# Retention states computed a head ahead, and three projections left beside the first attention scores, in a one-core hybrid transformer layer

## The chip, the core and the metric

The kernel runs on one core of a Trainium2 chip. A core has a matrix engine (PE, with its own weight loader PEld), three engines for elementwise work (VectorE or DVE, ScalarE or ACT, GpSimd or POOL), a queue that issues most transfers (SyncE or SP), and 16 DMA engines. Every engine works through its own list of instructions in order and waits on semaphores. On-chip memory has 128 partitions; PE writes only into PSUM, eight banks of 128x512 32-bit values. The metric is device time in microseconds (us) of one execution.

## What is computed

One layer of a diffusion backbone: 1024 latent tokens and 256 context tokens of width 1024, everything in 32-bit floating point.

```python
h_lat = rms_norm(x, norm1_g) * (1 + sc1) + sh1          # and h_ctx from the context
rq, rk, rv, rg, dq, dk, dv = split(h @ w_in)            # 7 blocks of 512 columns
# retention: 4 heads, 2 directions, chunks of 128 tokens
scores = (qc @ kc.T) * intra
o = scores @ vc + (qc * q_dec) @ S
S = S * c_dec + (kc * k_dec).T @ vc
y_ret = silu(rg) * sum(group_norm(o, gn_g[d]) for d in (0, 1))
# differential attention: 4 heads, two score maps each
a = softmax(q1 @ k1.T) - lam * softmax(q2 @ k2.T)
y_diff = rms_norm(a @ v) * subln_g * (1 - lambda_init)
x = x + g1 * (concat(y_ret, y_diff) @ w_out)
x = x + g2 * (conv3(h2 @ w_up) gated @ w_down);  out = rms_norm(x) * final_g
```

The context's state comes first in each direction, so a latent chunk's state S depends on all chunks before it (direction 0) or behind it (direction 1).

## The kernel before

**Large products.** A 32-bit operand is split into a high and a low part; `passes` (L126) multiplies high by high, high by low and low by high, so a tile of 128x512 results over a depth of 1024 takes 24 matmuls, called passes here. Function `natural` (L387) makes tiles with tokens on the partitions, `transposed` (L442) tiles with features on the partitions. A block of `w_in` is streamed in four slices, split by ACT (`whi`) and DVE (`wlo`, L183).

**Order of the blocks.** dv (block 6), dk (5), rv (2), rk (1), rg (3), rq (0), dq (4). After a tile of q or k, `rotated` (L415) applies the rotary position code: ACT copies the tile to `xb` with the halves of each rotated group exchanged, DVE forms `xa = tile*cos`, `xb*sin`, and their sum. For heads of 64 features the exchange goes in four copies of 32 partitions, for 128 in two of 64. `split_store` (L408) then splits a dk or dq tile (`xhl`: a cast by ACT, a subtraction by DVE) and stores it to memory (`dq_d`, `dk_d`).

**Side work.** `beside(g, rate, due)` hangs a generator of small steps next to the large products: `tick` (L376) is called after each group of three passes, adds `rate`, and takes a step of the generator for each whole unit. A scheduler may still move single instructions; the built order is fixed on each engine.

**Retention.** Beside block 3, `states_before` (L318) computes the direction-1 states of all four heads (nine products `pub` a head, DVE accumulates them into `Sb`). Beside blocks 0 and 4, `outputs` (L351) runs 32 steps (4 heads x 8 chunks). A step's instructions are spread over several iterations: POOL scales the query for both directions (`qq`, L256) and the key (`ks`, L231); PE forms the scores `pc` (L272); DVE masks them (`sc`, L274); PE forms the output `po` (four matmuls, L279 and L280) and the state product `puf` (L291), which DVE adds to the running direction-0 state `Sf` (L238) that the next step's `po` needs; ACT copies `po` to `o` and sums its squares (L282, L286); DVE adds the epsilon (`ss`, L114) and POOL raises to -0.5 (L115); DVE scales `o` twice (L297); POOL adds the directions and applies the gate (`y`, L299, L300); PE turns `y` (`pyt`, L304), ACT and DVE split it (`yr`, L309, L310), and every second step a transfer writes `yrd`.

**Attention.** A unit is one head and 128 queries, 32 in all. For each of its two score maps: six matmuls into `pA` (three banks, one such buffer for a map), a minimum over 1280 keys by DVE (`mt`, L731), an exponential by ACT (`p`, L735). Then DVE forms a ratio and combines the maps in place (L743); PE transposes ten blocks (`pt`), ACT copies them (`aT`), PE multiplies with the values (`pv`, L760, ten instructions that each show as two). The list `TAU` orders the operations of overlapping units, and `in_order` (L117) fixes that order on PE, DVE, ACT and SP. Below, a *score set* is one unit's six score matmuls for one map.

**The seam.** All retention steps are drained before the last `TAIL = 2` products of block 4. The buffers of the attention lie where the retention's lay, so the first loads `qhl`, `ks` (keys of head 0, in four parts, those of map 1 first) and `va`, issued by POOL, wait for the last `yrd` transfer. Unit 0's early operations (`EARLY`) stand in the program ahead of the last two products; their order is left to the scheduler.

Of the kernel before, what the change touches and what calls it, by code (L numbers as in the profile page):

```python
# [60 lines left out]
TAIL = 2  # L61
EARLY = ("S1", "M1", "S0", "M0", "E1", "E0", "R", "C")
# [10 lines left out]
def kernel(  # L73
# [63 lines left out]
    dq_d = [dr.tile([2, 64, 2, L], F32, name=f"dq{h}") for h in range(H)]  # L137
    dk_d = [dr.tile([2, 64, 2, LK], F32, name=f"dk{h}") for h in range(H)]
# [13 lines left out]
    with ExitStack() as p1:  # L152
# [8 lines left out]
        ps_b = psx.enter_context(tc.tile_pool(name="psb1", bufs=3, space=PSUM))  # L161
        mm_tiles = itertools.cycle([ps_b] * 3 + [ps_a] * 2)

        def mm_tile(name):
            return next(mm_tiles).tile([P, 512], F32, name=name, tag="mm")
# [52 lines left out]
        def load_kvg(h, g, nm, n, bufs=4):  # L218
            kvg = rt.tile([P, 2 if nm == "c" else 3, 2, P], F32, name=f"kvg{nm}", bufs=bufs)
            nc.sync.dma_start(out=kvg[:, :n], in_=kvg_d[g][:, :n, :, h * P : (h + 1) * P])  # L220
            return kvg
# [6 lines left out]

        def kscale(k1, h, d):
            kk = rt.tile([P, P], F32, name=f"ks{d}")  # L230
            nc.gpsimd.tensor_scalar(out=kk, in0=k1, scalar1=kd[:, h, d : d + 1], scalar2=0.0, op0=ALU.mult, op1=ALU.add)  # L231
            return kk

        def state_step(dst, prev, pu, h, d):
            if prev is None:
                nc.vector.tensor_copy(dst, pu)
            else:
                nc.vector.scalar_tensor_tensor(out=dst, in0=prev, scalar=cd[:, d * H + h : d * H + h + 1], in1=pu, op0=ALU.mult, op1=ALU.add)  # L238

        class Step:  # L240
            def __init__(self, n):
                self.h, self.t = divmod(n, NT)
                h, t = self.h, self.t
                if t % 2 == 0:
# [3 lines left out]
                    steps["pair"] = (qk, load_kvg(h, t // 2 + 1, "f", 3))  # L248
                qk, kvg = steps["pair"]
                self.qT, self.kT = (qk[:, i, t % 2 * P : (t % 2 + 1) * P] for i in range(2))  # L250
                self.kn, self.v, self.sg = (kvg[:, i, t % 2, :] for i in range(3))
                self.S = None
# [3 lines left out]
                nc.gpsimd.tensor_tensor(out=self.qq, in0=self.qT.unsqueeze(1).to_broadcast([P, 2, P]), in1=qd[:, h], op=ALU.mult)  # L256

            def first_state(self):
                ctx, kk = steps["ctx"]
                pu = pst.tile([P, NTC, P], F32, name="puc", tag="tr")  # L260
                for c in range(NTC):
                    mm(pu[:, c, :], kk[:, c, :], ctx[:, 1, c, :], start=True, stop=True)
# [558 lines left out]
        for op in EARLY:  # L821
            units[0].run(op)
# [556 lines left out]
```

## Time and profile before

| what | us |
|---|---|
| median of 3 runs | 1448.55 |
| lowest and highest | 1448.17, 1450.31 |
| the profiled execution | 1441.0 |
| its span, from first to last instruction shown | 1439.2 |
| block 3 with the direction-1 states | 288 to 342 |
| blocks 0 and 4 with the 32 retention steps | 342 to 497 |
| attention's score and value products | 494 to 693 |

Stages are told by the source lines of the PE instructions. A row of a timeline gives start, duration, engine, line, operation, result and operands, a count, and in brackets the idle time just before it with what ended it. A row of windows gives for each engine the busy time in a stretch, then the granted PE clock (1.00 is full), the DMA engines' busy share and the rate in GB/s.

### The profile page before, as it was taken

To read this page: it belongs to the slowest core of one execution; us is meant where nothing else is said; L and a number is where in the kernel's file an instruction comes from. 1 tells how busy PE (TensorE), PEld (TensorE's weight loads), DVE (VectorE), ACT (ScalarE), POOL (GpSimd) and SP (SyncE) were. 2 spreads that over 40 slices of the span, in tenths; PEclk is the share of its full clock that TensorE was granted. 3 is DMA by queue.
4 is the path that set the end of the run, shared out by engine and by line. 5 is a ranking of instruction groups with operands and counts; after the bars stand their busy time and mean duration, and the time that the engine had idled before them with its cause. 6 is when DMAs were issued, how large, how long until landed. Compare 5 with 4: busy or idle time off the path is not lost.

```text
span 1439.2 us, 19420 instructions
## 1 busy us (share of the span) xinstructions
PE 1379.9 (96%) x6924; PEld 1141.9 (79%) x6924; DVE 1003.8 (70%) x1493; ACT 732.4 (51%) x1394; POOL 340.8 (24%) x451
## 2 busy tenths in 40 slices
PE   6999999999899899999999899999999999999996
PEld 2678787887777789999888677888888888888885
DVE  3565655333677598888346888878777777998457
ACT  3535512322456688998224655555555545455533
POOL 1210000022787323431002253322223230000001
PEclk9999999999999999999999999999999999999999
DMA  8557655466455767480511123223222224953224
GB/s 332 199 194 240 219 196 190 137 193 195 134 173 164 208 156 164 121 143 1 220 62 78 59 104 118 108 110 110 92 87 93 110 110 174 391 206 102 101 95 176
DMA packets 107673, 218.30 MB, mean 152 GB/s; under 512 B 8948, under 2 KB 47348, under 8 KB 106680
## 3 DMA queue, kind: packets, MB, share of 16 engines
q1 hardware_dynamic: 99448, 192.14, 38.3%
q0 software_dynamic: 8128, 24.91, 7.7%
q8 instruction: 55, 0.90, 0.3%
q14 instruction: 42, 0.34, 0.1%
HBM read 159.61 MB, written 57.41 MB: 151 GB/s over the span
## 4 chain that ended last, share of the span: by engine, by line
PE 66%; DVE 8%; DMA 5%; POOL 3%; issue 3%; ACT 3%; SPq 0%; POOLq 0%; DVEq 0%; ACTq 0%
PE chain L129 5%; PE pv L760 5%; PE chain L130 5%; PE pA L728 5%; PE chain L131 5%; PE c L131 4%; PE c L129 4%; PE c L130 4%; PE third L130 2%; PE third L129 2%; PE third L131 2%; DMA W<-w_down 2%; PE pt L748 2%; PE pn L130 2%; PE pn L131 2%
## 5 line engine op out<-in xcount | busy, mean ns | idle before, releaser
L129 PE MATMUL chain<-T,whi 128*128 128x512 f32 x264 | 103.8, 394 | 4.9 <-ACT T L941 3.3
L129 PE MATMUL pl<-hT,whi 128*128 128x512 f32 x256 | 107.1, 419 | 0.0
L130 PE MATMUL chain<-T,whi 128*128 128x512 f32 x264 | 103.2, 391 | 0.0
L131 PE MATMUL chain<-T,wlo 128*128 128x512 f32 x264 | 102.6, 390 | 0.0
L131 PE MATMUL pl<-hT,wlo 128*128 128x512 f32 x256 | 100.5, 393 | 0.0
L130 PE MATMUL pl<-hT,whi 128*128 128x512 f32 x256 | 100.5, 393 | 0.0
L731 DVE TENSOR_REDUCE mt<-pA 128x1 f32<-128x1280 f32 x64 | 95.3, 1490 | 3.3 <-PE pA L728 1.5
L728 PE MATMUL pA<-ks,qhl 128*128 128x512 f32 (+1 forms) x384 | 91.6, 375 | 4.7 <-ACT p L735 4.7
L1024 POOL TENSOR_TENSOR cmb<-wrb 128x512 f32<-128x512 f32 x22 | 36.2, 1647 | 243.2 <-DMA wrb<-w_up 141.3
L131 PE MATMUL c<-whi,ghl 128*128 128x512 f32 x232 | 90.4, 390 | 0.2 <-DVE ghl L1183 0.2
L130 PE MATMUL c<-wlo,ghl 128*128 128x512 f32 x232 | 90.3, 389 | 0.0
L129 PE MATMUL c<-whi,ghl 128*128 128x512 f32 x232 | 90.2, 389 | 0.0
L115 POOL TENSOR_TENSOR sm<-sm,mhalf 128x1 f32<-128x1 f32 x26 | 16.1, 621 | 304.7 <-DVE sm L114 301.4
L735 ACT ACTIVATE p<-pA,mt 128x1280 f32<-128x1280 f32 x64 | 85.5, 1336 | 4.6 <-DVE mt L731 4.5
L894 ACT CAST whi<-cmb 128x512 fp32r<-128x512 f32 x66 | 41.0, 622 | 83.5 <-PE chain L130 63.7
L728 PEld LDWEIGHTS pA<-ks,qhl 128*128 128x128 f32 x384 | 68.9, 193 | 17.5 <-ACT p L735 5.8
L129 PE MATMUL pn<-whi,hT 128*128 128x512 f32 x192 | 79.1, 412 | 0.0
L760 PE MATMUL pv<-va,aT 128*128 128x128 f32 x640 | 77.0, 275 | 0.1
L131 PE MATMUL pn<-whi,hT 128*128 128x512 f32 x192 | 75.9, 398 | 0.5 <-DVE hT L540 0.5
L130 PE MATMUL pn<-wlo,hT 128*128 128x512 f32 x192 | 76.1, 396 | 0.0
L895 DVE TENSOR_TENSOR wlo<-cmb,whi 128x512 fp32r<-128x512 f32 x66 | 60.7, 922 | 20.2 <-ACT whi L894 20.2
L760 PEld LDWEIGHTS pv<-va,aT 128*128 128x128 f32 x640 | 74.0, 192 | 0.7 <-DVE yT L789 0.3
(301 smaller groups left out, 3884.1 us busy)
## 6 DMA issues: line engine op xcount, KB each, us to landing
wm<-w_mod SPq DMA_DIRECT2D x32, 512.0 KB, 4.4
raw<-w_in SPq DMA_DIRECT2D x28, 512.0 KB, 4.4
wra<-w_up SPq DMA_DIRECT2D x24, 512.0 KB, 3.2
wrb<-w_up SPq DMA_DIRECT2D x24, 512.0 KB, 3.5
W<-w_down SPq DMA_DIRECT2D x44, 256.0 KB, 6.4
ad<-s SPq DMA_DIRECT2D x20, 512.0 KB, 3.4
wra<-ad SPq DMA_DIRECT2D x20, 512.0 KB, 3.2
wrb<-ad SPq DMA_DIRECT2D x18, 512.0 KB, 3.3
```

The lines of the kernel that those rows point to most:

```text
L115: nc.gpsimd.tensor_tensor(out=out_ap, in0=out_ap, in1=mhalf[:, :n], op=ALU.pow)
L129: mm(ps, lh, rh, start=first, stop=False, skip_group_check=more)
L130: mm(ps, lh, rl, start=False, stop=False, skip_group_check=more)
L131: mm(ps, ll, rh, start=False, stop=last, skip_group_check=more)
L728: mm(self.pa[m][:, c0:c1], self.q[:, i, m, qs], self.k[:, m, c0:c1], start=(i == 0), stop=(i == 1))
L731: nc.vector.tensor_reduce(out=self.mt[:, m : m + 1], in_=self.pa[m][:, :LK], axis=AX.X, op=ALU.min)
L735: nc.scalar.activation(self.p[m], self.pa[m][:, :LK], AF.Exp, scale=-1.0, bias=self.mt[:, m : m + 1], accum_out=self.s[:, m : m + 1])
L748: nc.tensor.transpose(self.pt[g][:, i, :], self.p[0][:, (4 * g + i) * P : (4 * g + i + 1) * P], ident)
L760: mm(self.pv, self.aT[:, c, :], self.v[:, c, :], start=(c == 0), stop=(c == NKT - 1))
L894: nc.scalar.copy(hi, src)
L895: nc.vector.tensor_tensor(out=lo, in0=src, in1=r32(hi), op=ALU.subtract)
L1024: nc.gpsimd.tensor_tensor(out=s1, in0=b1, in1=b2, op=ALU.add)
```

## The change

**States.** `states_before` and the running direction-0 state are replaced by `states(h)`: 18 products of one head, both directions in turn, each chunk pair's keys and values loaded for each direction (`kvs`), keys scaled two chunks at a time (`ks`, 128x256). Heads 0 and 1 run beside block 3, head 2 during the steps of head 1, head 3 during those of head 2. The number of state products is unchanged (72), and so is that of scores, outputs and turns.

**Steps.** `outputs` scores two steps ahead instead of one (`qq` and `sc` get three buffers), has no state product of its own, loads values and gates alone, and DVE's epsilon instruction goes to POOL. The rate beside the products becomes 1.5 a tick after a delay of 21. PSUM: the three banks `psb1` are split into two more for the small results (five in all) and one for products (three in all).

**Seam.** `TAIL` is 3. The early operations of units 0 and 1 hang on the ticks of the last three products by the table `AHEAD`, and `in_order` fixes this stretch too. The load of the second half of head 0's queries waits for unit 1's combine.

**Exchange.** The host stores the columns of dq and dk with the two maps interleaved, so that the exchange is always two copies of 64 partitions; the memory layout of `dq_d`, `dk_d` and the rotary tables follow.

```diff
-TAIL = 2
-EARLY = ("S1", "M1", "S0", "M0", "E1", "E0", "R", "C")
+TAIL = 3
+EARLY = ("S1", "M1", "E1", "S0", "M0", "E0", "R", "C")
+AHEAD = {15: [(0, op) for op in EARLY[:3]], 18: [(0, op) for op in EARLY[3:6]], 22: [(1, op) for op in EARLY[:3]], 23: [(0, op) for op in EARLY[6:]], None: [(1, op) for op in EARLY[3:]]}
...
-                if t < NT - 1:
-                    self.kk = kscale(self.kn, h, 0)
-                self.qq = rt.tile([P, 2, P], F32, name="qq")
+                self.qq = rt.tile([P, 2, P], F32, name="qq", bufs=3)
...
-                rsqrt(self.ss, self.ss, 1.0, GN_EPS * P, 2)
-
-            def update(self, nxt):
-                pu = pst.tile([P, P], F32, name="puf", tag="tr")
-                mm(pu, self.kk, self.v, start=True, stop=True)
-                nxt.S = rt.tile([P, P], F32, name="Sf")
-                state_step(nxt.S, self.S, pu, self.h, 0)
+                nc.gpsimd.tensor_scalar(out=self.ss, in0=self.ss, scalar1=1.0, scalar2=GN_EPS * P, op0=ALU.mult, op1=ALU.add)
+                nc.gpsimd.tensor_tensor(out=self.ss, in0=self.ss, in1=mhalf[:, :2], op=ALU.pow)
...
+        def states(h):
+
+            seq = [(0, 0, (0, 1)), (1, 0, (1, 0))]
+            for g in range(1, 5):
+                seq += [(0, g, (0, 1) if g < 4 else (0,)), (1, 5 - g, (1, 0) if g < 4 else (1,))]
...
+                nc.gpsimd.tensor_scalar(out=ks, in0=kv[:, 0], scalar1=kd[:, h, d : d + 1], scalar2=0.0, op0=ALU.mult, op1=ALU.add)
...
+                for c in cs:
+                    pu = tr_tile([P, P], "pu")
+                    mm(pu, ks[:, c, :], kv[:, 1, c, :], start=True, stop=True)
...
+                        nc.vector.scalar_tensor_tensor(out=dst, in0=last[d], scalar=cd[:, d * H + h : d * H + h + 1], in1=pu, op0=ALU.mult, op1=ALU.add)
+                    last[d] = dst
+                    yield
...
-            for n in range(-2, n_steps + 4):
-                new = 0 <= n + 1 < n_steps
-                if new:
-                    steps[n + 1] = Step(n + 1)
-                    steps[n + 1].score()
+            lead = 2
+            more = iter(())
+            for n in range(-lead, n_steps + 4):
+                if n + lead < n_steps:
+                    steps[n + lead] = Step(n + lead)
+                    steps[n + lead].score()
...
+                if n == NT:
+                    more = states(2)
+                if n == 2 * NT:
+                    more = states(3)
...
+                for _ in range(3 if n % NT < 6 else 0):
+                    if next(more, more) is None:
+                        yield
...
-            for q in range(P // blk):
-                o = (q ^ 1) * blk
-                nc.scalar.activation(xb[q * blk : (q + 1) * blk, :], pt[o : o + blk, :], AF.Copy, scale=scale)
+            for q in (0, 64):
+                nc.scalar.activation(xb[q : q + 64, :], pt[64 - q : P - q, :], AF.Copy, scale=scale)
...
-        beside(outputs(), 1.2, -12.0)
+        beside(outputs(), 1.5, -21.0)
...
-        for op in EARLY:
-            units[0].run(op)
+        units[1] = Unit(1)
+        vars(units[1]).update(fore[1])
+
+        def prologue():
+            for k in range(8 * TAIL):
+                for u, op in AHEAD.get(k, ()):
+                    units[u].run(op)
+                yield
+
+        start = len(nc.cur_bb.bb.instructions)
+        beside(prologue(), 1.0)
         transposed(wg, dq_d, rtab, 32, -DIFF_SCALE, 0, by_head[-TAIL:])
+        for u, op in AHEAD[None]:
+            units[u].run(op)
+        in_order(start)
...
-                with tc.issue_after(units[n - 5].pool_ins.ins) if n >= 5 else nullcontext():
+                after = units[n - 5].pool_ins if n >= 5 else units[1].joined if n else None
+                with tc.issue_after(after.ins) if after else nullcontext():
                     fore.append(load(n + 3))
```

**POOL in the retention steps.** One step's instructions as they stand in a run of steps of head 0, before (from one power of -0.5, `ss<-ss,mhalf`, to the next):

```order
L115 TENSOR_TENSOR ss<-ss,mhalf 128x2
L299 TENSOR_TENSOR y<-o 128x128
L300 TENSOR_TENSOR y<-y,kvgf 128x128
L256 TENSOR_TENSOR qq<-qk,qd 128x256
L231 TENSOR_SCALAR ks_3241<-kvgf,kd 128x128
```

and now, at the border of head 0 and head 1, where the scaling of keys for head 2 begins:

```order
L267 TENSOR_SCALAR ss<-ss 128x2
L268 TENSOR_TENSOR ss<-ss,mhalf 128x2
L274 TENSOR_TENSOR y<-o 128x128
L275 TENSOR_TENSOR y<-y,kvo 128x128
L248 TENSOR_TENSOR qq<-qk,qd 128x256
L305 TENSOR_SCALAR ks<-kvs,kd 128x256
```

The epsilon instruction is new on POOL, the scaled keys are fewer and twice as wide; the first `y` still stands right behind the power of its own step.

**DVE at the seam.** `mt` is the minimum for one score set, `xa`, `xb`, `xhl` belong to the last two dq products, `p` is a unit's combine. Before, from unit 0's first minimum to unit 1's second (`pA_4584` and `pA_4592` are unit 0's maps 1 and 0, `pA_4711` and `pA_4721` unit 1's):

```order
L731 TENSOR_REDUCE mt_4582<-pA_4584 128x1
L412 TENSOR_TENSOR xhl_4642<-xa_4633,xhl_4642 128x512
L739 RECIPROCAL r_4604<-sa_4583 128x1
L731 TENSOR_REDUCE mt_4582<-pA_4592 128x1
L423 SCALAR_TENSOR_TENSOR xa_4671<-pl_4646,rtab_3830 128x512
L424 TENSOR_TENSOR xb_4672<-xb_4672,rtab_3830 128x512
L731 TENSOR_REDUCE mt_4709<-pA_4711 128x1
L740 SCALAR_TENSOR_TENSOR r_4604<-r_4604,sa_4583,nlam_145 128x1
L425 TENSOR_TENSOR xa_4671<-xa_4671,xb_4672 128x512
L743 SCALAR_TENSOR_TENSOR p0_4602<-p1_4600,r_4604,p0_4602 128x1280
L412 TENSOR_TENSOR xhl_4680<-xa_4671,xhl_4680 128x512
L731 TENSOR_REDUCE mt_4709<-pA_4721 128x1
```

and now, from behind unit 0's first minimum and the rotation of the product before the last, to unit 1's second minimum (`pA_4562` is unit 0's map 0, `pA_4584` and `pA_4612` unit 1's maps 1 and 0, `pA_4656` unit 2's map 1):

```order
L396 TENSOR_TENSOR xhl_4548<-xa_4541,xhl_4548 128x512
L720 TENSOR_REDUCE mt_4466<-pA_4562 128x1
L720 TENSOR_REDUCE mt_4468<-pA_4584 128x1
L728 RECIPROCAL r_4597<-sa_4467 128x1
L729 SCALAR_TENSOR_TENSOR r_4597<-r_4597,sa_4467,nlam_145 128x1
L732 SCALAR_TENSOR_TENSOR p0_4570<-p1_4539,r_4597,p0_4570 128x1280
L406 SCALAR_TENSOR_TENSOR xa_4601<-pl_4552,rtab_3750 128x512
L407 TENSOR_TENSOR xb_4602<-xb_4602,rtab_3750 128x512
L720 TENSOR_REDUCE mt_4654<-pA_4656 128x1
L408 TENSOR_TENSOR xa_4601<-xa_4601,xb_4602 128x512
L396 TENSOR_TENSOR xhl_4608<-xa_4601,xhl_4608 128x512
L720 TENSOR_REDUCE mt_4468<-pA_4612 128x1
```

Unit 0's second minimum has moved behind the rotation of the product before the last, and unit 1's second minimum now stands behind unit 2's first as well as behind the last product's rotation. On PE the score sets are unit 0's two and unit 1's map 1, with 9, 12 and 3 passes of the last product behind them; before, unit 0's map 1 alone stood ahead of the last ten passes.

More of the change, by code (lines that the diff above doesn't have):

```diff
@@ L253, in __init__ @@
[L253 to L268 removed]
+                self.v, self.sg = (kv[:, i, t % 2, :] for i in range(2))
@@ L302, in turn @@
             def turn(self):
-                pt = pst.tile([P, P], F32, name="pyt", tag="tr")
+                pt = tr_tile([P, P], "pyt")
                 nc.tensor.transpose(pt, self.y, ident)
```

146 lines of the change are left out of this document (64 added, 82 removed).

## The prediction

> **What bounds the kernel now.** First the page's head:
>
> ```profile
> span 1439.2 us, 19420 instructions
> PE 1379.9 (96%) x6924; PEld 1141.9 (79%) x6924; DVE 1003.8 (70%) x1493; ACT 732.4 (51%) x1394; POOL 340.8 (24%) x451
> ```
>
> PE is idle for 59 us in all, so a change that leaves PE its work can win only idle time, stage by stage. Next the view of windows, cut at the first retention scores (358.5), the last turn (477.8), the first score set (493.8) and the first value product (513.9); after the stretch and its length stand PE, PEld, DVE, ACT and POOL, then the granted clock:
>
> ```profile
> 300.00:350.00 50.00, 50.00 (x250) 41.62 (x249) 15.19 (x35) 9.55 (x13) 12.68 (x31) 1.00 0.58 182
> ```
> ```profile
> 342.00:358.50 16.50, 14.28 (x64) 11.29 (x63) 6.76 (x9) 5.08 (x7) 0.00 (x0) 1.00 0.68 218
> 358.50:477.80 119.30, 109.37 (x667) 91.83 (x668) 84.35 (x229) 65.25 (x225) 94.03 (x157) 1.00 0.48 154
> 477.80:493.80 16.00, 16.00 (x73) 13.20 (x72) 7.84 (x14) 10.69 (x18) 6.03 (x9) 1.00 0.92 199
> 493.80:513.90 20.10, 15.38 (x68) 12.33 (x66) 16.96 (x21) 12.12 (x20) 2.61 (x6) 0.83 0.68 209
> 513.90:542.50 28.60, 28.60 (x216) 26.85 (x215) 25.69 (x35) 25.44 (x60) 8.95 (x19) 1.00 0.75 167
> ```
>
> Two stages hold idle PE that the change touches: the retention steps (119.3 us, PE short of work for 9.9) and the attention's start (20.1 us, short for 4.7 and slowed by a clock of 0.83). Once the first value product runs, PE is full, so whatever the start loses stays lost. In the retention stage POOL is busy for 94.0 of 119.3. The waits there, and one period of POOL:
>
> ```profile
> DVE o L297 <- POOL ss L115: 19.6, 21, 1.7
> POOL y L299 <- DVE o L297: 17.0, 25, 1.3
> ...
> PE po L279 <- DVE Sf L238: 5.8, 7, 1.5
> ```
> ```profile
> 401.10 0.46 POOL L299 TENSOR_TENSOR y<-o 128x128 f32<-128x128 f32 x1 [1.26 <-DVE o L297]
> 401.63 0.46 POOL L300 TENSOR_TENSOR y<-y,kvgf 128x128 f32<-128x128 f32 x1
> 402.05 0.73 POOL L256 TENSOR_TENSOR qq<-qk,qd 128x256 f32<-128x256 f32 x1
> 402.76 0.38 POOL L231 TENSOR_SCALAR ks<-kvgf,kd 128x128 f32<-128x128 f32 x1
> 403.10 0.70 POOL L115 TENSOR_TENSOR ss<-ss,mhalf 128x2 f32<-128x2 f32 x1
> 404.53 0.46 POOL L299 TENSOR_TENSOR y<-o 128x128 f32<-128x128 f32 x1 [0.73 <-DVE o L297]
> ```
>
> PE names the state (`Sf`) as what it waits for, 5.8 us. But DVE stands still for 19.6 us until POOL's power is ready, and POOL then for 17.0 until DVE has scaled `o`: a period of 404.53 - 401.10 = 3.43 us, which 32 times is 110, near the stage's length. The pace is set by the pair POOL and DVE as much as by the state chain.
>
> **The change part by part.** The profiled execution took 1441.0 with a span of 1439.2, and the three runs' median is 1448.55: sums are made against the profiled one, and the difference is added to the median.
>
> *The retention steps.* PE's products are the same in number: 240 passes instead of 242 between the first scores and the last turn, as many small products. So PE's own pace stays 109.4, and only the wait can move. POOL's rows:
>
> ```profile
> L256 POOL TENSOR_TENSOR qq<-qk,qd 128x256 f32<-128x256 f32 x30 | 25.6, 853 | 2.7 <-PE po L280 2.0 <-POOL ks L231 0.5
> ...
> L231 POOL TENSOR_SCALAR ks<-kvgf,kd 128x128 f32<-128x128 f32 x26 | 12.5, 480 | 0.9 <-DMA qk<-rqk 0.9
> L348 POOL TENSOR_SCALAR kvgc<-kvgc,kd 128x256 f32<-128x256 f32 x3 | 2.0, 670 | 0.0
> ```
> ```profile
> L771 POOL TENSOR_TENSOR e<-sa 128x1 f32<-128x1 f32 x32 | 6.1, 193 | 21.2 <-ACT p L735 21.1
> ```
>
> Removed are 28 key scalings of 0.480 (13.4) and four of 0.670 (2.7); added 20 of the wide form at 0.670 (13.4) and 32 epsilon instructions over two columns. The trace has no such one on POOL: at least the 0.193 of the smallest elementwise row (6.2 in all), at most the 0.480 of the same operation over 128 columns (15.4); I take the first, being nearest in size. POOL's work becomes 94.0 - 16.1 + 19.6 = 97.5. Its idle time is 119.3 - 94.0 = 25.3. Of that, the pause between a power and its own `y` remains: the built order has them adjacent in 16 of 32 steps before and after, 16 x 0.73 = 11.7. The other 13.6, from the state chain and DVE's part of the epsilon, may go wholly or not at all; I take half, 6.8. The stage then lasts 97.5 + 25.3 - 6.8 = 116.0, so **-3.3**, with PE's own 109.4 (-9.9) and 97.5 + 25.3 = 122.8 (+3.5) as ends.
>
> *The states of heads 0 and 1* run beside block 3, where PE is never idle and POOL works 12.68 of 50 us; the same 36 products stand there, so this costs nothing; uncovered, the 20 wide key scalings would cost 13.4. The 12 further loads are hidden by DMA engines busy for 0.48 of the retention stage. Three PSUM banks instead of five for products leave each 16 us before it is needed again (three products of 24 passes); emptying one takes 1.2 us of copies and one 0.69 us DVE pass.
>
> *The exchange in two copies.* An ACT copy costs the same for 32 and for 64 partitions, so a dk or dq tile saves half of 2.39 us on ACT. PE works beside nearly all of these. One place is not covered, the start of block 2:
>
> ```profile
> 168.78 2.39 ACT L420 ACTIVATE xb<-pl 32x512 f32<-32x512 f32 x4
> 171.19 1.04 ACT L182 CAST whi<-raw 128x1024 fp32r<-128x1024 f32 x1
> ```
> ```profile
> 172.29 0.73 PE L129 MATMUL pn<-whi,cT 128*128 128x512 f32 x2 [1.11 <-ACT whi L182]
> ```
>
> The cast could come 1.2 earlier if its data were there, which the rows don't show: between 0 and -1.1, taken as **-0.5**.
>
> *The attention's start.* Three things. First, **the keys come too late**.
>
> ```profile
> 477.50 0.33 PE L304 MATMUL pyt<-ident,y 128*128 128x128 f32 x1 [0.26 <-POOL y L300]
> ```
> ```profile
> 482.21 0.84 POOL L806 DMA_DIRECT2D qhl<-dq  x1 [4.77 <-DMA yrd<-yr]
> ```
> ```profile
> L810 POOL DMA_DIRECT2D ks<-dk x2: 636/636/637, 483.7 to 484.2; - x2
> ...
> DMA to landing us min/median/max: 8.1/8.6/9.0
> ```
> ```profile
> 493.79 0.40 PE L728 MATMUL pA<-ks,qhl 128*128 128x512 f32 x1
> ```
>
> From the last turn to the first score set are 71 passes in 16.3 us (0.229 each). The second part of map 1's keys lands at 484.2 + 9.0 = 493.2, that is 15.7 after the last turn, just in time. In the changed order only 56 passes stand between, 12.8 us, while turn, split, store and loads are the same: PE waits 15.7 - 12.8 = **+2.9** (ends 0, if the transfers run faster, and 4).
>
> Second, **unit 1's second minimum waits behind both rotations**. Durations:
>
> ```profile
> 501.82 0.69 DVE L423 SCALAR_TENSOR_TENSOR xa<-pl,rtab 128x512 f32<-128x512 f32 x1 [0.87 <-ACT xb L420]
> ...
> 503.03 1.49 DVE L731 TENSOR_REDUCE mt<-pA 128x1 f32<-128x1280 f32 x1
> ...
> 505.16 1.55 DVE L743 SCALAR_TENSOR_TENSOR p<-p,r,p 128x1280 f32<-128x1280 f32 x1
> ```
> ```profile
> 504.55 1.33 ACT L735 ACTIVATE p<-pA,mt 128x1280 f32<-128x1280 f32 x1 [1.31 <-DVE mt L731]
> 505.77 0.19 ACT L735 ACTIVATION_READ_ACCUMULATOR p<-pA,mt 128x1 f32 x1
> 505.87 0.61 ACT L411 CAST xhl<-xa 128x512 fp32r<-128x512 f32 x1
> ```
> ```profile
> 497.25 1.30 PE L728 MATMUL pA<-ks,qhl 128*128 128x512 f32 x6
> ```
> ```profile
> 513.90 2.40 PE L760 MATMUL pv<-va,aT 128*128 128x128 f32 x20
> ```
>
> Count from the end f of the first score set, in the built order, with 1.45 a minimum, 1.5 an exponential, 1.2 the two copies, 0.6 to 0.7 each other rotation part. Minimum f+1.45, exponential 2.95, copies 4.15, three DVE parts 6.05, cast 6.7, subtraction 7.35; unit 0's second minimum 8.8, unit 1's first 10.25, its exponential 11.85; the last product's copies 13.05, two DVE parts 14.3; unit 2's first minimum 15.75, its exponential 17.2, cast 17.85, subtraction 18.5; unit 1's second minimum 19.95, exponential 21.5. Only then are unit 2's second scores free to start, and after two score sets (1.25 each) and eight transposes the first value product comes at f + 25.0. From the end of the product before the last that is 1.25 + 25.0 = 26.25, with PE work of 24 passes (5.5), seven score sets (8.7) and 14 transposes (1.35): 10.7 lost. Now: from 497.25 to 513.90 16.65 pass, with six sets and 14 transposes (8.8): 7.85 lost. So **+2.9**. Its ends: 0 and 5.
>
> Third, the gap of some 7 us before those scores **lowers the clock**. The window's row after that start (columns as above), and the landing of the first two query loads:
>
> ```profile
> 505.00:510.00 5.00, 3.81 (x13) 2.99 (x12) 5.00 (x5) 2.73 (x5) 0.00 (x0) 0.50 0.27 105
> ```
> ```profile
> DMA to landing us min/median/max: 5.8/6.5/7.3
> ```
>
> With less idle time than that the clock was 0.50 for about 5 us; here such a stretch would fall on the work right before the value product, costing half of it. The load of the second half of the queries has the same end: it waits for unit 1's combine (f + 23.5) and its second part lands 0.8 + 7.3 later, 2.6 after unit 4's scores could begin at f + 29.0. The two overlap, so once **+2.5** (ends 0 and 5).
>
> **Sum**: -3.3 - 0.5 + 2.9 + 2.9 + 2.5 = +4.5. That is 1443.7 for the span and 1453.0 for the median.
>
> **Rivals.** *The start is covered* (faster): the two score sets moved ahead of the last passes are what counts, and the start loses no more than now. For it: three sets instead of one stand beside products. Against it: both rows above, keys at 15.7 and DVE's order. Price: -3.3 - 0.5 = -3.8, so 1444.7. It decides if unit 1's second minimum ends before about f + 15.
>
> *PE sets the pace of the retention steps*: freed of the state, PE runs through, the stage lasts 109.4. For it: PE's own waits name the state. Against it: POOL's 3.43 us period, which the change leaves. -9.9 - 0.5 + 8.3 = -2.1: 1446.4.
>
> *The states were not what held the steps up* (the change doesn't do what it says): all 25.3 of POOL's idle time stays, the stage grows to 122.8. +3.5 - 0.5 + 8.3 = +11.3: 1459.9. For it: the adjacent power and `y`; against it: 5.8 us of PE waits that must vanish.
>
> *The epsilon instruction is blocked by DVE.* The rows: `qq` took 0.73 in the quiet period above and 0.853 on average, so POOL's instructions are stretched at times.
>
> ```profile
> L297 DVE SCALAR_TENSOR_TENSOR o<-o,ss,gn 128x128 f32<-128x128 f32 x62 | 23.7, 416 | 19.5 <-POOL ss L115 19.2
> ```
>
> If each of the 32 new ones waited for one such DVE instruction (0.416), POOL would gain 13.3 more: +4.5 + 13.3 = +17.8, so 1466.4. The Trainium skill, "SBUF — State Buffer", section "SBUF: two separate sides", says that DVE instructions with two SBUF inputs and GpSimd share a port pair that one holds for its whole instruction while the other blocks; by that rule moving work from DVE to POOL is bad here, and the stretched `qq` agrees in kind, though a mean of 17% speaks for an occasional block, not for one each time.
>
> **How the numbers follow.** Forecast 0.34, start covered 0.30, PE sets the pace 0.15, states not the holdup 0.15, blocked epsilon 0.06. About 0.2% (2.9 us) is what a measurement here can tell from no change. With some 2.5 us of play, the forecast is slower in 0.27 and the same in 0.07; the first rival faster in 0.22, same 0.06, slower 0.02; the second 0.07, 0.06, 0.02; the third slower in 0.14, same 0.01; the fourth slower in 0.06. Together faster 0.29, same 0.20, slower 0.51. The forecast's own range is 1449.5 to 1456.5; the range over the cases runs from 1442.0, below the first rival's time, to 1460.0, the third's, and leaves out the fourth and the faster tail.
>
> **What would show it.** Right: a PE wait of about 3 us for a transfer before the first score set, a gap of 5 to 8 us before unit 2's second scores with a clock near 0.5 after it, and 113 to 119 us from the first retention scores to the last turn. Wrong: a stage under 111 us with POOL's pauses gone; a first value product within 23 us of the first score set; a first score set without a wait for the keys.

## The result, and the profile after

The changed kernel took 1467.86 us (median of 6 runs, 1463.97 to 1470.90), against 1448.36 for the kernel before (median of 6 runs, 1442.11 to 1450.31). The ratio is 1.0143, with a 95% interval of 1.0123 to 1.0163: by it 20.7 us slower (19.5 by the medians), where 4.5 were forecast. The measured time lies outside the predicted range of 1442.0 to 1460.0.

The head of the page of the changed kernel:

```profile
span 1469.1 us, 19387 instructions
PE 1390.3 (95%) x6924; PEld 1150.7 (78%) x6924; DVE 995.9 (68%) x1461; ACT 714.7 (49%) x1362; POOL 337.6 (23%) x455
```

The two profiled spans differ by 29.9 us, more than the medians: the one of before (1441.0) is faster than its six runs, and this one (1470.9) is the slowest of its own. The view of windows tells where the time went, cut as in the prediction: first retention scores (now 360.0), last turn (492.7), first score set (509.4), first value product (539.8). After the stretch and its length stand PE, PEld, DVE, ACT, POOL, the granted clock, the DMA share and the rate:

```profile
360.00:492.70 132.70, 112.42 (x663) 95.26 (x663) 76.40 (x200) 60.90 (x218) 97.94 (x178) 0.96 0.48 150
492.70:509.40 16.70, 13.12 (x58) 10.58 (x58) 6.13 (x10) 5.37 (x9) 5.75 (x9) 0.99 0.83 207
509.40:539.80 30.40, 21.39 (x81) 17.56 (x82) 18.19 (x21) 13.44 (x21) 2.59 (x6) 0.73 0.54 150
```

| stretch | before | changed | forecast |
|---|---|---|---|
| up to the first retention scores | 358.5 | 360.0 | 358.0 |
| retention steps, first scores to last turn | 119.0 | 132.7 | 115.7 |
| last turn to first score set | 16.3 | 16.7 | 15.7 |
| first score set to first value product | 20.1 | 30.4 | 26.25, and 2.5 for the clock |
| after it | 925.3 | 929.3 | 925.3 |

Two stretches carry the change: +13.7 in the retention steps and +10.7 from the last turn to the first value product. What comes after is the same work in the same order; in the fifteen other profiled executions of this study it lasted 925.1 to 927.0, so the 4 us there belong to this one execution.

**The steps.** The view of waits for 360.0 to 492.7, then a row of PE's own waits there (engine, line and who it waited for, then us in total, times, longest):

```profile
DVE o L272 <- POOL ss L268: 46.8, 29, 3.0
POOL y L274 <- DVE o L272: 20.8, 25, 2.0
PE pyt L279 <- POOL y L275: 8.0, 5, 3.5
```
```profile
PE po L259 <- DVE S L322: 2.3, 2, 1.4
```

The row of PE's wait for `y` in the steps before:

```profile
PE pyt L304 <- POOL y L300: 1.7, 2, 1.3
```

PE's wait for the state went from 5.8 us to 2.3, as the change intends. But DVE's wait for POOL's power went from 19.6 to 46.8, and PE now waits 8.0 for POOL's `y`, 1.7 before. POOL by groups, in the same stretch (count, busy us, mean ns, then the idle time ahead of them):

```profile
L268 POOL TENSOR_TENSOR ss<-ss,mhalf 128x2 f32<-128x2 f32 x32 | 22.3, 697 | 2.3
...
L274 POOL TENSOR_TENSOR y<-o 128x128 f32<-128x128 f32 x32 | 16.2, 506 | 22.5 <-DVE o L272 20.8 <-DMA kvo<-kvg 1.2 <-DMA rqk<-xa 0.5
...
L267 POOL TENSOR_SCALAR ss<-ss 128x2 f32<-128x2 f32 x32 | 8.1, 254 | 5.1 <-ACT jk L266 2.6
```

POOL is busy for 97.94 us; the prediction summed 97.5, so the sum of its work was met. Its idle time was not: 132.70 - 97.94 = 34.8, where 25.3 stood before and 18.5 were forecast. A step with state products, on POOL's timeline:

```profile
401.87 0.19 POOL L267 TENSOR_SCALAR ss<-ss 128x2 f32<-128x2 f32 x1
402.14 0.69 POOL L268 TENSOR_TENSOR ss<-ss,mhalf 128x2 f32<-128x2 f32 x1
402.83 0.48 POOL L305 TENSOR_SCALAR ks<-kvs,kd 128x256 f32<-128x256 f32 x1
403.79 0.46 POOL L274 TENSOR_TENSOR y<-o 128x128 f32<-128x128 f32 x1 [0.48 <-DMA kvo<-kvg]
404.32 0.46 POOL L275 TENSOR_TENSOR y<-y,kvo 128x128 f32<-128x128 f32 x1
404.92 0.73 POOL L248 TENSOR_TENSOR qq<-qk,qd 128x256 f32<-128x256 f32 x1
405.63 0.49 POOL L305 TENSOR_SCALAR ks<-kvs,kd 128x256 f32<-128x256 f32 x1
406.26 0.19 POOL L267 TENSOR_SCALAR ss<-ss 128x2 f32<-128x2 f32 x1
406.53 0.70 POOL L268 TENSOR_TENSOR ss<-ss,mhalf 128x2 f32<-128x2 f32 x1
```

From power to power 406.53 - 402.14 = 4.39 us. This is the period from the 11th of the 32 powers to the 12th; the same one lasted 3.95 before, and the mean of all 31 went from 3.59 to 4.01. What POOL does stands in one ring: the power releases DVE's `o`, `o` releases `y`, and behind `y` the queue brings the next step's query, keys, epsilon and power. An instruction added to this ring can lengthen the step; by how much, the runs below show.

**The start.** PE's timeline (the last score set, transposes and what else lies between are left out; the figure in brackets is the idle time ahead of the row):

```profile
509.36 2.47 PE L717 MATMUL pA<-ks,qhl 128*128 128x512 f32 x6 [3.58 <-issue]
...
522.47 4.14 PE L717 MATMUL pA<-ks,qhl 128*128 128x512 f32 x12 [2.54 <-ACT p L724]
...
533.73 2.50 PE L717 MATMUL pA<-ks,qhl 128*128 128x512 f32 x6 [6.46 <-ACT p L724]
...
539.77 2.40 PE L749 MATMUL pv<-va,aT 128*128 128x128 f32 x20
```

The last 6.46 us are the wait that the prediction derived. On DVE and ACT stand ahead of it:

```profile
526.65 1.49 DVE L720 TENSOR_REDUCE mt<-pA 128x1 f32<-128x1280 f32 x1 [0.29 <-PE pA L717]
528.05 0.68 DVE L408 TENSOR_TENSOR xa<-xa,xb 128x512 f32<-128x512 f32 x1
530.13 0.69 DVE L396 TENSOR_TENSOR xhl<-xa,xhl 128x512 fp32r<-128x512 f32 x1 [1.40 <-ACT xhl L395]
530.74 1.48 DVE L720 TENSOR_REDUCE mt<-pA 128x1 f32<-128x1280 f32 x1
```
```profile
532.26 1.33 ACT L724 ACTIVATE p<-pA,mt 128x1280 f32<-128x1280 f32 x1 [1.88 <-DVE mt L720]
```

Unit 2's first minimum, the rest of the rotation with its wait for ACT's cast, and only then unit 1's second minimum. And the clock, in windows behind the three waits:

```profile
510.00:512.50 2.50, 2.50 (x9) 2.07 (x8) 0.58 (x1) 0.00 (x0) 0.00 (x0) 0.53 1.05 359
522.50:525.00 2.50, 2.50 (x7) 2.12 (x8) 1.77 (x2) 2.46 (x4) 0.19 (x1) 0.52 0.00 0
```
```profile
530.00:535.00 5.00, 1.27 (x3) 1.08 (x4) 3.42 (x5) 1.79 (x4) 0.69 (x2) 0.50 0.27 105
535.00:540.00 5.00, 5.00 (x21) 4.42 (x21) 2.78 (x3) 2.04 (x4) 1.71 (x4) 0.53 0.65 208
```

Each of the three waits is followed by a stretch near half clock; the forecast counted one such stretch.

### The profile page after: what moved, and what is told of

It reads as the page before. It is cut to its first block, busy times and chain, and to the rows that moved or that the text cites. A ratio compares the mean times of both kernels' runs of the same rounds, so it can differ in the third digit from the quotient of the medians.

```text
span 1469.1 us, 19387 instructions
## 1 busy us (share of the span) xinstructions
PE 1390.3 (95%) x6924; PEld 1150.7 (78%) x6924; DVE 995.9 (68%) x1461; ACT 714.7 (49%) x1362; POOL 337.6 (23%) x455
## 4 chain that ended last, share of the span: by engine, by line
PE 55%; DVE 5%; DMA 2%; issue 2%; ACT 1%; POOL 1%; POOLq 0%; DVEq 0%
PE pA L717 5%; PE chain L130 5%; PE chain L131 5%; PE chain L132 5%; PE pv L749 5%; PE c L132 4%; PE c L131 4%; PE c L130 3%; PE third L131 3%; PE third L130 2%; PE third L132 2%; PE pt L737 2%; PE po L130 2%; PE po L131 2%; PE po L132 2%
## 5 line engine op out<-in xcount | busy, mean ns | idle before, releaser
L717 PEld LDWEIGHTS pA<-ks,qhl 128*128 128x128 f32 x384 | 71.2, 199 | 25.9 <-ACT p L724 9.7
```

What stands on the lines that cost most here:

```text
L717: mm(self.pa[m][:, c0:c1], self.q[:, m, i, qs], self.k[:, m, c0:c1], start=(i == 0), stop=(i == 1))
```

## The experiments

Fourteen variants were run beside the kernel before. Two lengths are read from each profile: the retention steps, and the time from the last turn to the first value product, called the start below. Lengths of one profiled execution have some play: three profiles with the steps of before and the start of before or after give 119.0, 121.8 and 120.6 for the same steps.

| kernel | steps | start | ratio to before, 95% interval |
|---|---|---|---|
| before | 119.0 | 36.4 | 1 |
| changed | 132.7 | 47.1 | 1.0143 [1.0123, 1.0163] |
| changed start alone | 121.8 | 46.4 | 1.0074 [1.0057, 1.0091] |
| changed retention alone | 131.9 | 35.9 | 1.0079 [1.0064, 1.0094] |
| changed, epsilon on DVE | 123.7 | 45.6 | 1.0100 [1.0081, 1.0118] |
| changed, states spread | 133.9 | 46.1 | 1.0157 [1.0126, 1.0188] |
| before, epsilon on POOL | 133.1 | 36.7 | 1.0101 [1.0077, 1.0125] |
| before, one more POOL instruction | 128.2 | 36.9 | 1.0070 [1.0047, 1.0092] |
| before, 64-row exchange | 120.6 | 36.3 | 1.0001 [0.9985, 1.0018] |
| changed, minimum first | 132.7 | 42.7 | 1.0125 [1.0095, 1.0154] |
| minimum first, four ticks later | 133.1 | 38.7 | 1.0095 [1.0073, 1.0117] |
| the same with epsilon on DVE | 125.5 | 39.1 | 1.0057 [1.0036, 1.0078] |
| changed retention, epsilon on DVE, keys on ACT | 119.2 | 36.0 | 0.9988 [0.9971, 1.0006] |
| even ticks, epsilon on DVE | 126.8 | 36.1 | 1.0028 [1.0009, 1.0047] |
| even ticks, epsilon on DVE, keys on ACT | 121.3 | 36.8 | 0.9992 [0.9974, 1.0009] |
| the same, begun later | 122.8 | 36.4 | 0.9984 [0.9966, 1.0002] |

### Two halves: the start alone, the retention alone

The first has `TAIL = 3`, the table `AHEAD`, the fixed order and the 64-row exchange on top of the retention of before; the second has the changed retention and the exchange with `TAIL = 2` and unit 0 alone.

> The changed start of the attention (three products left, two units begun, 64-row exchange) with the retention steps of before. Theory A (the loss has two separate parts: retention steps +13 us and start +10 us, as the trace of the change shows them): steps at 119 to 120 us as before, first score set to first value product about 30 us, total 8 to 12 us over before. Theory B (the start is late only because the stretched retention steps deliver late): start back near 20 us and total within 3 us of before.

> The changed retention (states a head ahead, epsilon on POOL) with the old start (two products left, one unit begun). Theory A: steps 130 to 133 us, start back to 20 us, total 10 to 15 us over before. Theory C (the steps are long only because of what is drained into the last three products): steps at 122 us or less, total within 4 us of before.

The steps of the retention alone and the start of the start alone, in their windows:

```profile
359.80:491.70 131.90, 112.99 (x664) 95.76 (x665) 77.09 (x200) 60.96 (x218) 97.94 (x178) 0.96 0.49 151
```
```profile
500.70:530.40 29.70, 21.18 (x80) 16.99 (x81) 17.77 (x21) 13.44 (x21) 2.59 (x6) 0.74 0.52 154
```

The loss is two losses, each there without the other (0.74% and 0.79%; the two together measured 1.43%). Theories B and C fall.

### The epsilon instruction

```diff
-                nc.gpsimd.tensor_scalar(out=self.ss, in0=self.ss, scalar1=1.0, scalar2=GN_EPS * P, op0=ALU.mult, op1=ALU.add)
+                nc.vector.tensor_scalar(out=self.ss, in0=self.ss, scalar1=1.0, scalar2=GN_EPS * P, op0=ALU.mult, op1=ALU.add)
```

> The change with the epsilon instruction back on DVE. Theory D (the 32 epsilon instructions sit in POOL's serial chain, 0.25 us and a gap of 0.08 each): steps shorter by 8 to 11 us, about 122 to 125, total the same amount below the change. Theory E (key scalings and state updates bunched in 16 steps make the loss, the epsilon is off the path): steps shorter by less than 3 us.

Its rival, in the changed kernel, with the 18 states of a head spread over eight steps:

```diff
-                for _ in range(3 if n % NT < 6 else 0):
+                for _ in range(2 + (n % NT < 2)):
```

> The change with the 18 state products of a head spread over eight steps (3, 3, then 2 each) instead of three in each of six. Theory E (bunching): steps shorter by 5 us or more, below 128. Theory D (epsilon in the chain of every step): steps within 2 us of the change's 132.7.

The steps of the one and of the other:

```profile
360.90:484.60 123.70, 108.15 (x663) 91.42 (x663) 84.01 (x232) 60.63 (x218) 88.74 (x146) 1.00 0.51 160
```
```profile
357.40:491.30 133.90, 112.06 (x664) 94.79 (x665) 77.20 (x200) 61.60 (x218) 97.97 (x178) 0.97 0.48 149
```

The epsilon back on DVE: 9.0 us shorter, and POOL's busy time fell by 97.94 - 88.74 = 9.2 with its idle time where it was (35.0). (In all, four profiles with the changed steps give 131.9 to 133.1, two with the epsilon on DVE 123.7 and 125.5.) The total fell by less than the 8 to 11 us expected, 0.43% or 6.2 us by the ratios, whose intervals don't overlap. Spreading the states: no gain. Theory D holds; E falls in the form tested, 18 products over eight steps instead of six. (The last of these sections shows that the steps with state products hold a loss all the same.) Then the same edit the other way round, alone, in the kernel before:

```diff
-                rsqrt(self.ss, self.ss, 1.0, GN_EPS * P, 2)
+                nc.gpsimd.tensor_scalar(out=self.ss, in0=self.ss, scalar1=1.0, scalar2=GN_EPS * P, op0=ALU.mult, op1=ALU.add)
+                nc.gpsimd.tensor_tensor(out=self.ss, in0=self.ss, in1=mhalf[:, :2], op=ALU.pow)
```

> The kernel before with nothing changed but the epsilon instruction, moved to POOL. Theory D (POOL's queue sets the pace of the steps and the epsilon adds its 0.25 us and two gaps of 0.08 to every step): steps 127 to 130 us instead of 119, total 8 to 11 us over before. Theory F (it costs that only together with the wide key scalings of the change): steps under 122, total within 3 us of before.

Windows and waits of this kernel:

```profile
362.60:495.70 133.10, 114.50 (x665) 94.90 (x665) 76.53 (x197) 65.57 (x225) 101.58 (x189) 0.96 0.43 138
```
```profile
DVE o L298 <- POOL ss L288: 43.2, 27, 3.2
```

One small instruction a step, moved from one engine to another with nothing else touched, costs 14.1 us of steps and 1.01% of the whole: as much as the whole changed retention, and more than the 127 to 130 us of steps and the 8 to 11 in total that D expected. D holds in kind and F falls. It left open whether POOL's queue is full as such, or the place between ACT's squares and the power is what hurts. So an instruction of the same form was put behind the scaled query, with a result that nobody reads, and the epsilon stayed on DVE:

```diff
+                junk = rt.tile([P, 2], F32, name="junk")
+                nc.gpsimd.tensor_scalar(out=junk, in0=self.qq[:, 0, :2], scalar1=1.0, scalar2=GN_EPS * P, op0=ALU.mult, op1=ALU.add)
```

> The kernel before with one more POOL instruction per step of the epsilon's form (128x2, its result used by nothing) right behind the scaled query, the epsilon itself staying on DVE: it adds work to POOL's queue and nothing to the way from the squares to the power. Theory D (POOL's queue time is the pace): steps 127 to 133 us, as with the epsilon moved. Theory M (the moved epsilon costs because it stands between ACT's squares and the power that DVE waits for, not because POOL is full): steps 119 to 122 us.

```profile
364.40:492.60 128.20, 113.12 (x666) 94.43 (x667) 84.63 (x229) 65.28 (x225) 100.60 (x189) 0.97 0.45 143
```
```profile
L258 POOL TENSOR_SCALAR junk<-qq 128x2 f32<-128x2 f32 x32 | 8.4, 261 | 2.8
```
```profile
DVE o L299 <- POOL ss L115: 27.6, 26, 2.3
```

Steps longer by 9.2 us: POOL's busy time grew by 100.60 - 94.03 = 6.6 and its idle time by the other 2.6. So an instruction in POOL's queue costs time though nobody reads its result, as theory D says, and M's 119 to 122 us is missed. The epsilon itself cost 14.1, some 5 us more, and there DVE waits 43.2 us for the power, here 27.6: this fits a further cost of its place, theory M. It isn't shown, because unchanged steps varied by 2.8 us between profiles and the intervals of the two ratios overlap.

A part of these costs is PE's clock. Windows of 0.25 us show stretches at half clock in the steps of the changed kernel, of the epsilon moved alone and of the useless instruction, and none in those of before or with the epsilon back on DVE. PE's busy time times the missing share of the clock comes to 4.4, 5.0 and 3.4 us. These stretches follow waits of PE, so they belong to the price of the longer ring; how much of them held the steps up is not separated.

### The start

The minimum first: unit 1's second scores, minimum and exponential hang on the last tick, ahead of the last rotation.

```diff
-AHEAD = {... 23: [(0, op) for op in EARLY[6:]], None: [(1, op) for op in EARLY[3:]]}
+AHEAD = {... 23: [(0, op) for op in EARLY[6:]] + [(1, op) for op in EARLY[3:6]], None: [(1, op) for op in EARLY[6:]]}
```

> The change with unit 1's second scores, minimum and exponential put ahead of the last rotation instead of behind it. Theory G (that minimum, behind the rotation and unit 2's first minimum, makes the 6.5 us wait of PE and half a clock after it): first score set to first value product 22 to 26 us instead of 30.4, total 5 to 8 us below the change. Theory H (the start is slow because too few passes are left to cover two units): 28 us or more.

Then, with that edit kept, the operations hung on the ticks 19, 21 and 23:

```diff
-AHEAD = {15: [(0, op) for op in EARLY[:3]], 18: [(0, op) for op in EARLY[3:6]], 22: [(1, op) for op in EARLY[:3]], 23: ...
+AHEAD = {19: [(0, op) for op in EARLY[:3]], 21: [(0, op) for op in EARLY[3:6]], 23: [(1, op) for op in EARLY[:3]] + ...
```

> The change with the minimum put first and all early operations hung four ticks later (19, 21, 23 instead of 15, 18, 22), so that 68 passes instead of 56 stand between the last turn and the first score set. Theory K (the time from the keys' landing to the first value product is one chain of minima and exponentials, and passes only fill it): the wait for the keys goes, but last turn to first value product stays at 42.7 +- 1.5 us, because 12 fewer passes fill the chain behind it. Theory L (the wait for the keys is a loss of its own): 3 to 4 us shorter, 39 to 40.

The stretch from first score set to first value product of the first, and what PE waits for at its start; then the second's:

```profile
511.30:537.20 25.90, 20.27 (x81) 16.62 (x82) 16.95 (x20) 11.92 (x19) 0.38 (x2) 0.81 0.51 136
```
```profile
PE pA L717 <- DMA dq<-xhl: 3.8, 1, 3.8
```
```profile
511.80:534.00 22.20, 15.39 (x68) 12.33 (x69) 14.97 (x17) 10.74 (x17) 0.38 (x2) 0.85 0.60 160
```
```profile
PE pA L717 <- DMA dq<-xhl: 0.7, 1, 0.7
```

The order of the one minimum is worth 4.5 us of this stretch (30.4 to 25.9), so G holds for the start: 42.7 lies below all four profiles with the old order, 45.6 to 47.1. The total shows less, 1.0125 against 1.0143 with overlapping intervals, where 5 to 8 us were expected. Covering the loads with 12 more passes is worth another 4.0 (42.7 to 38.7): K falls, L holds, and 1.0095 is clear of 1.0143. The wait for the loads is a loss of its own: it shrank by 3.8 - 0.7 = 3.1, and the clock of the stretch behind it rose from 0.81 to 0.85. Both edits bring the start to within 2.3 us of before.

### Both repairs, and the exchange

> The change with the two edits that the runs so far point to: the epsilon back on DVE (9.0 us of the steps) and the minimum first with the early operations four ticks later (8.4 us of the start). If these two account for the loss and do not lean on each other: steps 122 to 125 us, last turn to first value product 38 to 40 us, total 3 to 7 us over before. If one repair undoes the other (the earlier steps leave the start with less cover): 8 us or more over before.

The steps took 125.5 us and the start 39.1, 0.57% over before: one instruction's engine and the order of the start, with no change to what is computed, take back 0.86 of the 1.43%. Both lengths are as expected to within half a microsecond, so the repairs do not undo each other. The total, 7.9 us over by the medians (1451.16 and 1443.3), is above the 3 to 7 expected and just under the 8 given to the rival: against the profile of before, 6.5 us in the steps and 2.7 in the start are still missing.

> The kernel before with the 64-row exchange and its memory layout alone. Covered nearly everywhere: 0 to -1.1 us against before. If the two copies of 64 rows shorten the rotations in the retention steps and the start: -2 to -4 us.

Ratio 1.0001: the exchange in two copies is worth nothing that can be measured, which agrees with the first expectation; the 2 to 4 us of the second are not seen.

### Do the states ahead gain anything?

With the epsilon on DVE the steps still took 123.7. POOL's 32 powers, one a step, tell where. Their starts on POOL's timeline cut the steps into three parts (lengths in us):

| kernel | powers 1 to 10 | powers 10 to 22 | PE busy in these | powers 22 to 32 |
|---|---|---|---|---|
| before | 31.9 | 44.0 | 41.0 | 35.3 |
| changed | 33.2 | 56.2 | 49.8 | 34.9 |
| changed, epsilon on DVE | 29.4 | 54.7 | 49.4 | 31.7 |
| before, epsilon on POOL | 34.9 | 49.8 | 42.8 | 38.5 |
| even ticks, epsilon on DVE | 34.5 | 48.2 | 42.8 | 35.1 |

The middle part holds the state products of heads 2 and 3, and the ticks give PE more passes there too: 109 rows of passes in the changed kernel, 89 before. With the epsilon on DVE the outer parts are 2.5 and 3.6 us shorter than before, so the steps that have lost their state do gain. The middle part is 10.7 longer, and there PE's work alone, 49.4, exceeds the whole 44.0 of before. The epsilon costs 7.0 us in the outer parts and 1.5 in the middle one.

The next runs keep the epsilon on DVE and the start of before. They took POOL's key scalings to ACT (`nc.scalar.mul(ks, kv[:, 0], kd[:, h, d : d + 1])`), and gave each step the same three ticks at a rate of 1.2:

```diff
-                yield
-                if not NT <= n < 3 * NT:
-                    yield
-                for _ in range(3 if n % NT < 6 else 0):
-                    if next(more, more) is None:
-                        yield
+                next(more, None)
+                yield
+                next(more, None)
+                if n % NT < 2:
+                    next(more, None)
+                yield
```

> The changed retention with the old start, the epsilon back on DVE and the key scalings moved from POOL to ACT: POOL loses 9.1 us of work against the run with the epsilon on DVE. Theory D (POOL's queue is the pace): steps 112 to 116 us, total 4 to 10 us below before. Theory I (what is left of the loss is PE's uneven number of passes in a step and its waits for the turn): steps 121 to 124 us, total at or above before.

> The changed retention with the old start, the epsilon back on DVE, and every step given the same number of ticks (3 at a rate of 1.2, the states hung two or three to a step within them). Theory I (what was left, 123.7 us, comes from light steps of 6 passes in which PE outruns POOL and heavy ones of 9 in which all engines are late): steps 115 to 120 us. Theory J (POOL's waits for DVE's queue, longer by the state updates, set it whatever the passes): steps 122 to 125 us.

> The same with the key scalings on ACT instead of POOL. Theory I: PE sets the pace, 110 to 114 us, total 5 to 9 us below before. Theory J: no shorter than the 119.2 us of the run with key scalings on ACT and uneven ticks.

> The changed retention with even ticks, the epsilon on DVE, the key scalings on ACT, the old start, and the steps begun two ticks later at a rate of 1.25, so that the 4.9 us wait for the second query tile goes. Theory I: steps 112 to 116 us, total 3 to 7 us below before. Theory J: 119 us or more, total within 2 us of before or above.

Without the key scalings POOL is busy for 80.64 us only, and the steps took 119.2, so 4.5 came back: theory D expected 112 to 116, theory I 121 to 124, and neither has it. Even ticks alone gave 126.8, outside both expectations: they took 6.5 us from the middle part and added 8.6 to the outer ones. PE's waits there show a new one:

```profile
PE pc L251 <- DMA qk<-rqk: 6.8, 2, 4.9
PE pyt L278 <- POOL y L274: 3.8, 3, 2.0
```

The steps run into the second tile of the queries before it has landed. With even ticks and the key scalings on ACT the steps took 121.3, as theory J said. With the steps begun after 14 ticks instead of 10 (four later, not two as the expectation says; `beside(outputs(), 1.25, -18.0)`) as well, PE's waits for the queries were still 4.5 us in all, the longest 2.7, and the kernel took 0.9984 of before, [0.9966, 1.0002], which is not clearly faster. So this last test of theories I and J is undecided: the one profile with 122.8 us speaks for J, the ratio for a gain of 0 to 5 us. No variant was clearly better than the kernel before.

## Why the prediction was wrong, point by point

**What bounds the kernel.** Right for the two stages, and for the pair POOL and DVE in steps without state products. The prediction said that the pace is set by this pair "as much as by the state chain", and its sum then took half of the idle time beyond one kind of pause as free.

**The retention steps: this step failed.** Forecast -3.3, with +3.5 as its upper end; measured +13.7. The term that fell is "of that, the pause between a power and its own `y` remains ... the other 13.6 may go wholly or not at all; I take half": POOL's idle time was taken as something that can only shrink, so that the new work would be paid for by the pauses. Instead it grew from 25.3 to 34.8.

The runs show two things in its place. First, the pauses did not pay for the epsilon: with it back on DVE the steps were 9.0 us shorter, POOL's work 9.2 less and its idle time the same. In a ring of two in-order engines a pause can be one engine's wait for the other, and an instruction added to one half lengthens the ring. Second, the idle time grew with the rest of the change, for it stayed at 35.0 without the epsilon. The prediction counted PE's products over the whole stage ("PE's own pace stays 109.4") and not where they stand. In the twelve middle periods PE had 49.8 us of work, and POOL's idle time went from 6.9 to 13.1. With the epsilon on DVE 4.7 us were left over before, about the balance of 10.7 lost in these periods and 6.1 won in the others. What sets the length of the middle part beyond PE's 49.4 us is not shown.

The sum of POOL's work (97.94 for 97.5) was met in part by luck: the wide key scalings took 9.4 us in 18 rows where 13.4 were summed, and the epsilon 8.1 where 6.2 were. Its price of 0.193 each was low: the mean is 0.254, with 26 of the 32 at 0.19 to 0.20. Counted as part of the ring, 0.19 and a gap of 0.08 in each of 32 steps are 8.6, near the 9.0 that putting it back returned. That is a match in total only: by parts it was 0.37 a period in the outer 19 and 0.12 in the middle 12, and in the kernel before the same move cost 14.1.

**The states a head ahead.** That they go beside block 3 for nothing is borne out within the play of that time: the time up to the first scores moved by 1.5 us in this profile and lay between 357.0 and 364.5 in all others, with or without them. PE's waits for the state went from 5.8 to 2.3 as said. The time came back only in the steps without state products. With the epsilon on DVE PE still waited for POOL's `y`, for 5.5 us instead of the 1.7 of before:

```profile
PE pyt L279 <- POOL y L275: 5.5, 5, 2.0
```

The key scalings are a part of what is left (4.5 us with them on ACT); no run has both the gain of the outer parts and a middle part as short as before.

**The exchange.** Forecast -0.5, measured 1.0001 [0.9985, 1.0018]: not contradicted, and too small to tell.

**The keys.** Forecast +2.9; PE stood for 3.58 us. Right. The profile names no transfer for this wait, and in the two kernels with the minimum first it names the store of the queries; that it is the keys rests on the times. The second part of map 1's keys was issued at 499.9 and landed 9.0 us later, 0.4 before the first score set.

**Unit 1's second minimum.** Mechanism right: the wait stands where it was derived (6.46 us, within the 5 to 8 named), and the order alone gave back 4.5. From the end of the first set, 509.36 + 2.47 = 511.83, to the first value product it is 539.77 - 511.83 = 27.9 against the 25.0 counted, which held no half clock.

**The clock.** Mechanism right, its size too small: one stretch at half clock was counted, three came. By windows of 0.25 us half clock cost PE some 6.2 us between the last turn and the first value product, where 2.5 were counted. On the other side the waits behind the first score set were 2.54 + 6.46 = 9.0, where 10.7 were counted. So the three terms of the start sum to 8.3 and 10.7 were measured (10.0 with the changed start alone), and the excess is the clock's.

**The signs named ahead.** The wait before the first score set and the gap with a low clock behind it came; the 113 to 119 us for the steps did not.

**The rivals.** The start was not covered. The steps did not run at PE's 109.4, though PE's work fills most of the middle part. The third had the right side, with 3.5 of the 13.7 us. The fourth gave 1466.4, near the 1467.86 measured, and named the right instruction, but the number is near by luck, for its mechanism is not what the trace shows: only 6 of the 32 epsilon instructions were longer than 0.21 us, 2.0 us in all, where it asked for 13.3. The Trainium skill, "SBUF — State Buffer", section "SBUF: two separate sides", says that a DVE instruction with two SBUF inputs and a GpSimd instruction that reads SBUF share a port pair which one of them holds for its whole length. The trace agrees in kind, with 6 stretched instructions of 32, each beside a DVE instruction that reads two tiles from SBUF, and not in the size that the rival gave it.

## What to carry to other kernels

Where two in-order engines wait for each other in every step, sum the ring from one release to the next, not each engine's busy time: an instruction of 0.19 us moved onto it cost 9.0 us in one kernel and 14.1 in the other, over 32 steps. That POOL is busy for 24% of the span says nothing of the stage, where it was at 79%. Sum by parts of a stage as well: work moved within it, at the same total, lost 10.7 us where it went and won 6.1 where it had been. And in an order written by hand, the operation that frees a buffer for the next large product goes ahead of work that nobody waits for: one minimum moved in front of a rotation was worth 4.5 us of its stretch.

## What was not expected of the hardware

A wait of PE of 2.54 us was enough for a stretch near half clock (0.52 from 522.5 to 525.0). In the kernel before it was one of 2.44:

```profile
503.29 1.75 PE L728 MATMUL pA<-ks,qhl 128*128 128x512 f32 x6 [2.44 <-ACT p L735]
```

The Trainium skill, "TensorE: Matmul & The Clock Gate", section "Part 1: The HAM clock gate (the "warmup" mystery)", puts the fall to half clock behind an idle window of about 3.4 us; here waits of 2.44 us before and 2.54 us after the change sufficed. In the steps shorter ones did: 1.89 us in the changed kernel, and 1.34 with the useless instruction (one of 0.94 stood three us ahead of it). A wait of 2.22 at the first scores of the kernel before was followed by none, so its length alone does not decide. Read in windows of 0.5 us, the stretches at half clock lasted 3.4 us, or 6.8 and 10.2 (twice and three times that). So a wait of PE can cost more than its length: half of a 3.4 us stretch in which PE is busy throughout, 1.7 us, is an estimate of what comes on top.
